# Half of the gate projections of a hybrid transformer layer, in pairs by one level of Strassen's method

## The chip, the cores and the metric

The kernel runs on one core of a Trainium2 chip. The metric is the device time of one execution in microseconds; lower is better. Engines are called by short names: PE (TensorE, matrix products), DVE (VectorE), ACT (ScalarE), POOL (GpSimd) and SP (SyncE, which issues the DMAs here).

## The reference

One layer on x of 1024 positions x 1024 channels, in float32. Cut to what matters here:

```python
proj = x @ w_in
q_a, k_a, v_a, f_a, q_b, f_b, i_b, g_b, gate_a, gate_b = split(proj)
y_a = fox_attention(q_a, k_a, v_a, log_sigmoid(f_a + b_f))       # 8 heads of 64
o_b = hgrn2_chunkwise(silu(q_b), 1 - f, i_b, log(f))             # 4 heads of 128, f from f_b
o_b = o_b * rsqrt(mean(o_b ** 2) + eps) * norm_g
y_b = o_b * sigmoid(g_b)
merged = sigmoid(gate_a) * (y_a @ w_pa) + sigmoid(gate_b) * (y_b @ w_pb)
x = layer_norm(ALPHA * x + merged @ w_o)
u, g = split(x @ w_ff_in)                                        # 2 x 2816 wide
x = layer_norm(ALPHA * x + (silu(g) * u) @ w_ff_out)
```

The change concerns gate_a and gate_b: two products of x (1024 x 1024) with a weight matrix of 1024 x 1024.

## The kernel before

Every product of float32 matrices is made of three matmuls on parts of reduced width: both factors are split into a high part, a cast on ACT, and a low part, the difference, on DVE (`split`, L337). `mm3` (L366) issues high x high, high x low and low x high into one PSUM bank. A matmul takes a 128x128 piece of a weight as the stationary operand and 512 positions of x^T as the moving one, so its result is a tile of 128 channels x 512 positions. The split parts of x^T (xh, xl) stay in SBUF from the start.

The stages are: the accumulations for v (va, vb); the projections and the attention of four pairs of heads; the projections and the recurrence of four heads of HGRN2 (`hgrn`, L613); the branch projections p_a and p_b with the merge (tiles pps); w_o and the first layer norm; the FFN; the second layer norm. The FFN already computes its first product by one level of Strassen's method (`chunk`, L1043): for two column blocks of 128 channels and two halves of 512 positions, seven products of half the contraction length with sums of operands, instead of eight. Its split weight parts (tiles Tp) rotate over six slots: four of tag kb, and wr0 and wr1 (TSLOTS, L975).

The gates are 16 projections: two sets (i = 0 for gate_a, 1 for gate_b) of KC = 8 blocks of 128 channels. `gate(n, lane)` (L766) does one: it loads the block's weights (tile wg_r, 512 KB), splits them in two parts of four k-chunks (wg_h, wg_l), runs `project` (L377) for either half of the positions, 8 chunks x 3 matmuls each into a bank gps, copies the bank to SBUF on ACT (tile gt) and stores it to gate_d in DRAM. The merge loads it back later (tile sg).

The order of everything is a planner's. The program first records all calls in the class Plan (L54 to L280), with the tiles that each needs. `schedule` then lists them greedily: at each step the call that can start earliest by the planner's own costs goes next, with ties to the one recorded first; a tile's slot must be free. `issue` emits the result at one line, which is why every row of the profile names L280. The gates are recorded last, behind the recurrence (L790), so those of set 0 go into PE's holes during attention and recurrence, and those of set 1 run one behind the other after the recurrence's last head. LATE (L29) gives the gates 8, 10, 12 and 14 lane 0 (weight tiles wr0, wh0, wl0 and bank g), the others lane 1 (bank h).

At the end of a head's recurrence (L741 to L762) the chain is: nb (the decays of the last level, DVE), a matmul lp_nb, two COPY_PREDICATED of the mask into the matrix at (DVE), the matmuls op, the squares with their sums on ACT (ob, ss), ss scaled on DVE, rr = ss to the power -1/2 on POOL, ob = op x rr on DVE, four transposes ot on PE, yb on DVE, and the store to yb_d. It is run for two halves.

Of the kernel before, what the change touches and what calls it, by code (L numbers as in the profile page):

```python
# [8 lines left out]
F32R = mybir.dt.float32r  # L9
# [7 lines left out]
P = 128  # L17
S = 1024
D = 1024
KC = D // P  # L20
# [3 lines left out]
NB = 512  # L24
# [1 line left out]
CHUNKS = [[(0, n)] if n <= NB else [(0, n - w), (n - w, w)] for n, w in  # L26
          ((128, 0), (256, 0), (384, 0), (512, 0), (640, 256), (768, 256), (896, 384), (1024, 512))]
WTAGS = ("qk",) * 6 + ("kb",) * 4 + ("pf",) * 4 + ("hl",) * 2
LATE = (8, 10, 12, 14)  # L29
MERGE = {"g": "s"}  # L30
SPREAD = {"s": 2, "pt": 2, "pv": 1, "g": 1, "h": 2}
LOOSE = ("ps_s", "gt", "ps_h")
# [251 lines left out]
def trunk(ctx: ExitStack, tc, a: dict, out: bass.AP):  # L284
    nc = tc.nc
    plan = Plan(tc)
    sync, act, dve, pool, pe = (plan.queue(n, e) for n, e in (
        ("SP", nc.sync), ("ACT", nc.scalar), ("DVE", nc.vector), ("POOL", nc.gpsimd), ("PE", nc.tensor)))
# [13 lines left out]
    def bank(tag, name):  # L302
        tag = MERGE.get(tag, tag)
        return plan.tile(ps, [P, NB], F32, "ps_" + tag, name, BANKS[tag])

    def take(tag, shape, name, dt=F32):
        return plan.tile(root, [P] + shape, dt, tag, name, BUFS[tag])

    def full(tag, name, dt=F32):
        return take(tag, [S], name, dt)  # L310

    def half(tag, name, dt=F32):
        return take(tag, [NB], name, dt)
# [14 lines left out]
    def hs(i):  # L328
        return slice(i * NB, (i + 1) * NB)
# [4 lines left out]
    def f(ap):  # L334
        return ap.bitcast(F32)

    def split(hi, lo, src):  # L337
        act.copy(hi, src)
        dve.tensor_sub(lo, src, f(hi))
# [3 lines left out]
    def lane_of(lane):  # L343
        if lane is None:
            lane = turn[0]
            turn[0] ^= 1
        return lane
# [6 lines left out]
    def weights(src, shape, name, lane=None):  # L354
        lane = lane_of(lane)
        raw = raw_load(src, shape, name, lane)

        n = shape[0] // 2
        parts = []
        for i in range(2):  # L360
            hi, lo = (take(f"w{x}{lane}", [n] + shape[1:], f"{name}_{x}{i}", F32R) for x in "hl")
            split(hi, lo, raw[:, i * n:(i + 1) * n])
            parts.append((hi, lo))
        return [tuple(t[:, c % n] for t in parts[c // n]) for c in range(shape[0])]

    def mm3(o, lh, ll, rh, rl, first, last, more={}):  # L366
        mm(o, lh, rh, start=first, stop=False, **more)
        mm(o, lh, rl, start=False, stop=False, **more)
        mm(o, ll, rh, start=False, stop=last, **more)

    xh = [take("x", [4, S], f"xh{i}", F32R) for i in range(2)]
    xl = [take("x", [4, S], f"xl{i}", F32R) for i in range(2)]

    def X(c):
        return xh[c // 4][:, c % 4, :], xl[c // 4][:, c % 4, :]
# [10 lines left out]
    stage = ["qk"] * 6 + ["kb"] * 2  # L386
# [3 lines left out]
    for c2 in range(KC // 2):  # L390
# [12 lines left out]
        lane = lane_of(None)  # L403
        for j in range(2):
            c = 2 * c2 + j
            wh, wl = (take(f"w{n}{lane}", [NB], f"wva{c}_{n}", F32R) for n in "hl")
            h, l = X(c)
# [27 lines left out]
    for t in range(NT):  # L435
        vb = half(("tt", "ph")[t % 2], f"vb{t}")
        o = [bank(("pt", "h")[t % 2], f"vb_acc{t}_{i}")[:, :HV] for i in range(2)]
        for i in range(2):
            r = slice(i * HV, (i + 1) * HV)
            for c in range(KC):  # L440
                h, l = X(c)
# [322 lines left out]
    gate_d = dram.tile([2, KC, P, S], F32, name="gate_d")  # L764

    def gate(n, lane):  # L766
        i, fb = divmod(n, KC)
        plan.early = EARLY
        w = weights(a["w_g"][i, fb], [KC, P], f"wg{i}_{fb}", lane)
        plan.early = 0  # L770
        for hf in range(2):
            o = bank("gh"[lane], f"gps{i}_{fb}_{hf}")
            project(o, w, hf)
            t = half("gt", f"gt{i}_{fb}_{hf}")
            act.copy(t, o)
            sync.dma_start(gate_d[i, fb, :, hs(hf)], t)

    qk = qk_project(0)
    for p in range(4):
        attention(p, qk)  # L780
        if p < 3:
            qk = qk_project(p + 1)
# [3 lines left out]
    for h in range(HB):  # L786
        hgrn(h, qfg, box)
        if h < HB - 1:
            qfg = hgrn_project(h + 1)
    for n in range(2 * KC):  # L790
        gate(n, 0 if n in LATE else 1)


    UTAGS = ["qk"] * 6 + ["hl"] * 2 + ["kb"] * 4 + ["pf"] * 4
# [7 lines left out]
    for i, src in enumerate((ya_d, yb_d)):  # L802
# [6 lines left out]
        for fb in range(KC):  # L809
# [4 lines left out]
            w = [(hi[:, c], lo[:, c]) for c in range(4)]  # L814
            for hf in range(2):
# [3 lines left out]
                o = bank(CYC[nbank % 5], f"pps{i}_{fb}_{hf}")  # L819
# [92 lines left out]
    for t in range(NT):  # L912
# [16 lines left out]
        for g in range(2):  # L929
# [3 lines left out]
            if t < 4:  # L933
                h, l = (X11, X12)[g]
# [61 lines left out]
    class Chunk:  # L996
        def __init__(self, c, raw=None):
            self.c = c
            self.g, self.u = raw or (take("pf", [KC, P], f"w{n}{c}_r") for n in "gu")
            for i, t in enumerate((self.u, self.g)):  # L1000
                sync.dma_start(t, a["w_ff"][c, i])
            self.r = {}

        def sums(self, *names):
            g, u = self.g, self.u
            b11, b12, b21, b22 = g[:, :4], u[:, :4], g[:, 4:], u[:, 4:]
            for n in names:
                self.r[n] = take("tt", [4, P], f"t{n}_{self.c}")
                x, y = {"1": (b12, b11), "2": (b22, self.r.get("1")), "3": (b22, b12), "4": (b21, self.r.get("2"))}[n]
                dve.tensor_sub(self.r[n], x, y)  # L1010
# [15 lines left out]
    def mul(k, n, o, first, apart=False):  # L1026
        product(o, k.T(n, apart), OPS[n], first)
# [75 lines left out]
    for k, o in zip(ks, banks):  # L1103
        k.sums("3")
        mul(k, "p7", o[1], False)
        u3 = ring(f"u3_{k.c}")
# [51 lines left out]
    u = [half(("wh0", "wl0", "wh1", "wl1")[i], f"fu{i}") for i in range(4)]  # L1158
# [4 lines left out]
    for prod in ("p1", "p5", "p6", "p4", "p7", "p2"):  # L1163
# [3 lines left out]
        for g in range(len(GR)):  # L1167
            d, n = group(prod, ai[prod], g)
# [4 lines left out]
        for t in range(4):  # L1173
            o = acc[t]
# [29 lines left out]
    for t in range(4):  # L1204
# [5 lines left out]
        for i, s_ in enumerate(parts):  # L1210
            w = s_.stop - s_.start
            o = next_bank(f"p3_{t}_{i}")
# [100 lines left out]
```

## Time and profile before

| | |
|---|---|
| time, median of 3 runs | 1484.45 us (1484.18 to 1487.03) |
| the profiled execution | 1483.79 us |
| its span | 1482.0 us |
| mean granted PE clock | 0.998 |
| PE busy | 1464.2 us, 99% |
| DVE busy | 1005.8 us, 68% |
| ACT busy | 648.7 us, 44% |
| gates behind the recurrence | 569.65 to 656.80 us |

The profiled execution is one run of the program with the hardware profiler; its times belong together and lie near the median. A busy share is over the whole span. Matmuls overlap their neighbours, so the time that one adds is read from the starts of a dense row of them, not from the length of its record.

### The profile page before, as it was taken

The numbers are of one execution on the slowest core, as the hardware profiler recorded it, in microseconds if no ns is written. First come the engines' busy times: TensorE is split into PE (matmuls) and PEld (weight loads), VectorE is DVE, ScalarE is ACT, GpSimd is POOL, SyncE is SP. The second block draws the span as 40 slices with busy tenths as digits, with TensorE's granted clock in tenths as the row PEclk, the third lists the DMA queues.
The fourth block names the chain that finished last, engine by engine and source line by source line (L and its number), as shares of the span: only waits on it lengthen the run. The fifth ranks groups of instructions, "written<-read, shape, count | busy, mean of one in ns | idle before, by whom it ended". The sixth has DMA issues, their size and how long they took to land.

```text
span 1482.0 us, 19306 instructions
## 1 busy us (share of the span) xinstructions
PE 1464.2 (99%) x7081; PEld 1218.4 (82%) x7081; DVE 1005.8 (68%) x1913; ACT 648.7 (44%) x1101; POOL 95.6 (6%) x116
## 2 busy tenths in 40 slices
PE   9999999999999999999999899999999999999998
PEld 7997888888887888888888778888888888888887
DVE  5238676686887882134838897666666666798597
ACT  5127667677567653234511443233332333434330
POOL 0004132130101000000001000000000000000000
PEclk9999999999999999999999999999999999999999
DMA  6202212121211214346710304222233335976741
GB/s 241 77 33 83 69 55 77 42 75 40 78 36 57 67 63 142 107 157 222 265 52 1 114 22 136 97 95 98 102 106 107 107 107 175 342 265 226 250 160 58
DMA packets 78415, 170.68 MB, mean 115 GB/s; under 512 B 7400, under 2 KB 20328, under 8 KB 78320
## 3 DMA queue, kind: packets, MB, share of 16 engines
q1 hardware_dynamic: 78320, 169.44, 34.1%
q8 instruction: 56, 0.92, 0.3%
q14 instruction: 39, 0.32, 0.1%
HBM read 130.32 MB, written 39.09 MB: 114 GB/s over the span
## 4 chain that ended last, share of the span: by engine, by line
PE 94%; DVE 3%; ACT 1%; DMA 1%; issue 0%; POOL 0%; SPq 0%; DVEq 0%; ACTq 0%
PE p L280 14%; PE fb L280 11%; PE gps L280 11%; PE fc L280 8%; PE fa L280 8%; PE bps L280 8%; PE pps L280 6%; PE o L280 6%; PE vb_acc L280 3%; PE va_acc L280 3%; PE pv L280 2%; PE s L280 2%; PE qps L280 2%; PE kps L280 2%; PE pt L280 2%; PE lp L280 1%
## 5 line engine op out<-in xcount | busy, mean ns | idle before, releaser
L280 PE MATMUL p<-dp 128*128 128x512 f32 (+1 forms) x957 | 210.0, 382 | 0.0
L280 PEld LDWEIGHTS p<-dp 128*128 128x128 f32 x957 | 175.4, 188 | 34.7
L280 PE MATMUL fc<-xs,Tp 128*128 128x512 f32 x528 | 127.1, 390 | 0.0
L280 PE MATMUL fb<-xs,Tp 128*128 128x512 f32 x528 | 126.7, 390 | 0.0
L280 PEld LDWEIGHTS fc<-xs,Tp 128*128 128x128 f32 x528 | 99.1, 188 | 20.7 <-ACT xs L280 0.2
L280 PEld LDWEIGHTS fb<-xs,Tp 128*128 128x128 f32 x528 | 99.1, 188 | 20.6
L280 PE MATMUL fa<-x,Tp 128*128 128x512 f32 x480 | 115.8, 390 | 0.3 <-DVE u L280 0.3
L280 PEld LDWEIGHTS fa<-x,Tp 128*128 128x128 f32 x480 | 90.1, 188 | 19.3 <-ACT p L280 0.7
L280 ACT CAST Tp<-t 128x512 fp32r<-128x512 f32 x88 | 54.3, 620 | 116.4 <-PE fc L280 71.9
L280 DVE TENSOR_TENSOR Tp<-t,Tp 128x512 fp32r<-128x512 f32 x88 | 60.6, 691 | 60.5 <-ACT Tp L280 60.0
L280 PE MATMUL gps<-xl,wg_h 128*128 128x512 f32 x256 | 101.4, 396 | 0.0
L280 PE MATMUL gps<-xh,wg_h 128*128 128x512 f32 x256 | 101.3, 396 | 0.0
L280 PE MATMUL gps<-xh,wg_l 128*128 128x512 f32 x256 | 100.9, 394 | 0.0
L280 ACT CAST dp<-dap 128x1024 fp32r<-128x1024 f32 (+1 forms) x42 | 41.2, 983 | 102.2 <-PE p L280 51.7
L280 PE MATMUL bps<-xh,wb_l 128*128 128x512 f32 x192 | 76.1, 397 | 0.0
L280 PE MATMUL bps<-xh,wb_h 128*128 128x512 f32 x192 | 76.0, 396 | 0.0
L280 PE MATMUL bps<-xl,wb_h 128*128 128x512 f32 x192 | 75.9, 396 | 0.0
L280 POOL TENSOR_TENSOR rstd<-ve,mhalf 128x1 f32<-128x1 f32 x16 | 14.6, 914 | 898.1 <-DVE ve L280 898.1
L280 DVE TENSOR_TENSOR tl<-pt,th 128x512 fp32r<-128x512 f32 (+1 forms) x96 | 50.7, 552 | 20.2 <-ACT th L280 20.0
L280 DVE TENSOR_TENSOR wg_l<-wg_r,wg_h 128x512 fp32r<-128x512 f32 x32 | 22.5, 704 | 57.8 <-ACT wg_h L280 57.8
L280 DVE TENSOR_TENSOR dp<-dap,dp 128x1024 fp32r<-128x1024 f32 (+1 forms) x42 | 47.5, 1133 | 15.2 <-ACT dp L280 15.2
L280 PE MATMUL fb<-x,Tp 128*128 128x512 f32 x240 | 57.7, 389 | 0.0
(282 smaller groups left out, 3339.8 us busy)
## 6 DMA issues: line engine op xcount, KB each, us to landing
dbp<-in_w_fo SPq DMA_DIRECT2D x45, 512.0 KB, 5.2
dap<-a_d SPq DMA_DIRECT2D x35, 512.0 KB, 4.6
a_d<-ar SPq DMA_DIRECT2D x42, 256.0 KB, 3.8
wu_r<-in_w_ff SPq DMA_DIRECT2D x20, 512.0 KB, 3.7
wg_r<-in_w_ff SPq DMA_DIRECT2D x20, 512.0 KB, 3.6
a_d<-as SPq DMA_DIRECT2D x33, 256.0 KB, 2.3
wg_r<-in_w_g SPq DMA_DIRECT2D x16, 512.0 KB, 3.6
gate_d<-gt SPq DMA_DIRECT2D x32, 256.0 KB, 2.4
```

The source lines that it names most:

```text
L280: getattr(q.engine, method)(*args, **kw)
```

## The change

The first 8 gates (PLAIN) stay as they were, all of them in lane 1. The other 8 are taken in four pairs of neighbouring blocks. With g and u the weights of the two blocks of a pair and q the quarters of x^T (two halves of the contraction, two halves of the positions), one level of Strassen's method (the variant with shared sums, as in the FFN) gives the four result tiles from seven products of 4 chunks x 3 matmuls. A product's weight operand is a sum of quarters of g and u (tiles tg, on DVE) or a quarter itself; it is split into Tg..h (ACT) and Tg..l (DVE), in the tiles of the old gates' weight parts (tags wh0, wl0, wh1, wl1, two buffers each). The lanes alternate from product to product. The moving operand of p1, p2 and p4 is a quarter of xh, xl. For p5, p6, p7 and p3 the sums of quarters (gs1 to gs4) are made anew: x^T is loaded again in eight pieces of 512 KB (xg), added on DVE and split. The pairs 8 and 12 of the weights are named by their first block. The pairs 8 and 10 are worked jointly, product by product; the sums of x^T are made between. The pairs 12 and 14 follow in the FFN's order of products. The results are combined by copies on ACT (gp1, gt) and additions on DVE (gp1, gu2, gu3) and stored to gate_d as before.

```diff
@@ -26,7 +26,7 @@
 CHUNKS = [[(0, n)] if n <= NB else [(0, n - w), (n - w, w)] for n, w in
           ((128, 0), (256, 0), (384, 0), (512, 0), (640, 256), (768, 256), (896, 384), (1024, 512))]
 WTAGS = ("qk",) * 6 + ("kb",) * 4 + ("pf",) * 4 + ("hl",) * 2
-LATE = (8, 10, 12, 14)
+PLAIN = 8
 MERGE = {"g": "s"}
 SPREAD = {"s": 2, "pt": 2, "pv": 1, "g": 1, "h": 2}
 LOOSE = ("ps_s", "gt", "ps_h")
@@ -787,8 +787,144 @@
         hgrn(h, qfg, box)
         if h < HB - 1:
             qfg = hgrn_project(h + 1)
-    for n in range(2 * KC):
-        gate(n, 0 if n in LATE else 1)
+    for n in range(PLAIN):
+        gate(n, 1)
+    def operand4(tags, name):
+        ts = [[take(tags[2 * j + i], [2, NB], f"{name}{'hl'[i]}{j}", F32R) for j in range(2)] for i in range(2)]
+        return [[ts[i][c // 2][:, c % 2, :] for c in range(4)] for i in range(2)]
+    def operand1(tag, name):
+        t = take(tag, [2, 4, NB], name, F32R)
+        return [[t[:, i, c, :] for c in range(4)] for i in range(2)]
+    def quarter(i, m):
+        return [[x[i][:, c, hs(m)] for c in range(4)] for x in (xh, xl)]
+    gops = {"p1": quarter(0, 0), "p2": quarter(1, 0), "p4": quarter(1, 1)}
+    glane = [0]
+    class GatePair:
+        def __init__(self, n):
+            self.n = n
+            self.at = [divmod(n + j, KC) for j in range(2)]
+            self.w = []
+            for j in range(2):
+                t = take("kb", [KC, P], f"wg{n + j}_r")
+                sync.dma_start(t, a["w_g"][self.at[j]])
+                self.w.append(t)
+            (g, u), self.r = self.w, {}
+            self.src = {"p1": g[:, :4], "p2": g[:, 4:], "p3": u[:, 4:]}
+        def sums(self, *names):
+            g, u = self.w
+            for n in names:
+                t = take("tt", [4, P], f"tg{n}_{self.n}")
+                self.r[n] = t
+                x, y = {"1": (u[:, :4], g[:, :4]), "2": (u[:, 4:], self.r.get("1")), "3": (u[:, 4:], u[:, :4]),
+                        "4": (g[:, 4:], self.r.get("2"))}[n]
+                dve.tensor_sub(t, x, y)
+                self.src[{"1": "p5", "2": "p6", "3": "p7", "4": "p4"}[n]] = t
+        def mul(self, p, o, first):
+            lane = glane[0]
+            glane[0] ^= 1
+            T = [take(f"w{x}{lane}", [4, P], f"Tg{p}_{self.n}{x}", F32R) for x in "hl"]
+            split(*T, self.src[p])
+            more = {} if first else {"skip_group_check": True}
+            A = gops[p]
+            for c in range(4):
+                mm3(o, T[0][:, c], T[1][:, c], A[0][c], A[1][c], first and c == 0, c == 3, more)
+        def store(self, j, hf, t):
+            i, fb = self.at[j]
+            sync.dma_start(gate_d[i, fb, :, hs(hf)], t)
+        def stage(self, o):
+            t = half("gt", f"gt{self.n}_11")
+            act.copy(t, o)
+            self.store(0, 0, t)
+    pairs = [GatePair(n) for n in (PLAIN, PLAIN + 2)]
+    gbanks = [[bank(t, f"gs{k.n}_{i}") for i, t in enumerate(tags)] for k, tags in zip(pairs, (("h", "s", "s", "h"), ("s", "pv", "pt", "pt")))]
+    xr = []
+    for c in range(4):
+        two = [full(("wr0", "wr1")[j] if c == 0 else "qk", f"xg{c + 4 * j}_r") for j in range(2)]
+        for j in range(2):
+            sync.dma_start(two[j], a["xT"][c + 4 * j])
+        xr.append(two)
+    q11, q21, q12, q22 = ([x[j][:, hs(m)] for x in xr] for j, m in ((0, 0), (0, 1), (1, 0), (1, 1)))
+    def sums4(op, dst, x, y, sub):
+        for c in range(4):
+            (dve.tensor_sub if sub else dve.tensor_add)(dst[c], x[c], y[c])
+            split(op[0][c], op[1][c], dst[c])
+    for k, o in zip(pairs, gbanks):
+        k.mul("p1", o[0], True)
+        k.p1 = half("ph", f"gp1_{k.n}")
+        act.copy(k.p1, o[0])
+        k.mul("p2", o[0], False)
+        k.stage(o[0])
+        k.sums("1", "2", "4")
+        k.mul("p4", o[3], True)
+    gops["p5"] = operand1("x", "gs1")
+    sums4(gops["p5"], q22, q21, q22, False)
+    for k, o in zip(pairs, gbanks):
+        k.mul("p5", o[2], True)
+    gops["p6"] = operand1("m", "gs2")
+    sums4(gops["p6"], q22, q22, q11, True)
+    for k, o in zip(pairs, gbanks):
+        k.mul("p6", o[1], True)
+        k.u2 = half("ph", f"gu2_{k.n}")
+        dve.tensor_add(k.u2, o[1], k.p1)
+    gops["p7"] = operand4(("pf",) * 4, "gs3")
+    sums4(gops["p7"], q11, q11, q21, True)
+    for k, o in zip(pairs, gbanks):
+        k.sums("3")
+        k.mul("p7", o[1], False)
+        dve.tensor_add(k.p1, o[1], k.p1)
+        u3 = half("tt", f"gu3_{k.n}")
+        dve.tensor_add(u3, o[3], k.p1)
+        k.store(0, 1, u3)
+        dve.tensor_add(k.p1, o[2], k.p1)
+        k.store(1, 1, k.p1)
+    gops["p3"] = operand1("v", "gs4")
+    sums4(gops["p3"], q12, q12, q22, True)
+    for k, o in zip(pairs, gbanks):
+        k.mul("p3", o[2], False)
+        dve.tensor_add(k.u2, o[2], k.u2)
+        k.store(1, 0, k.u2)
+    G8 = ("h", "s", "s", "s", "h", "pt", "pv", "pt")
+    gb = 0
+    for n in range(PLAIN + 4, 2 * KC, 2):
+        k = GatePair(n)
+        ka, kb, kc = (bank(G8[(gb + i) % 8], f"gs{n}_{i}") for i in range(3))
+        gb += 3
+        p1, u2, u3 = (half("ph", f"g{x}_{n}") for x in ("p1", "u2", "u3"))
+        k.mul("p1", ka, True)
+        act.copy(p1, ka)
+        k.sums("1", "2")
+        k.mul("p6", kb, True)
+        dve.tensor_add(u2, kb, p1)
+        k.mul("p5", kc, True)
+        k.sums("3")
+        k.mul("p7", kb, False)
+        k.mul("p2", ka, False)
+        dve.tensor_add(u3, kb, p1)
+        k.sums("4")
+        k.mul("p4", kb, False)
+        dve.tensor_add(u3, kc, u3)
+        k.store(1, 1, u3)
+        k.stage(ka)
+        k.mul("p3", kc, False)
+        dve.tensor_add(p1, kb, p1)
+        k.store(0, 1, p1)
+        dve.tensor_add(u2, kc, u2)
+        k.store(1, 0, u2)
 
 
     UTAGS = ["qk"] * 6 + ["hl"] * 2 + ["kb"] * 4 + ["pf"] * 4
```

**The tail of the last head's recurrence, on DVE.** Before, the rows from the last difference nbp3 to the second ob3 are these (names end in the number of the buffer; wg0_7 are the weight parts of gate 7):

```order
L280 TENSOR_TENSOR nbp3_1285<-nbp3_1285,nbe3_1286 128x512
L280 TENSOR_TENSOR nb3_1284<-nbp3_1285,nb3_1284 128x512
L280 TENSOR_TENSOR wg0_7_l0_1365<-wg0_7_r_1363,wg0_7_h0_1364 128x512
L280 COPY_PREDICATED at3_1254<-lmask_172,lp3_nb_1287 128x4x64 x2
L280 TENSOR_TENSOR wg0_7_l1_1367<-wg0_7_r_1363,wg0_7_h1_1366 128x512
L280 TENSOR_SCALAR ss_1289<-ss_1289 128x4
L280 TENSOR_TENSOR ob3_0_1290<-op3_0_1288,rr_1291 128x512
L280 SCALAR_TENSOR_TENSOR yb3_0_1293<-ot3_0_1292,ng_173,hbg3_1228 128x512
L280 TENSOR_SCALAR ss_1295<-ss_1295 128x4
L280 TENSOR_TENSOR ob3_1_1296<-op3_1_1294,rr_1297 128x512
```

Now the piece up to the second part of the mask reads:

```order
L280 TENSOR_TENSOR gs1_1414<-xg5_r_1387,gs1_1414 128x512
L280 TENSOR_TENSOR nb3_1284<-nbp3_1285,nb3_1284 128x512
L280 TENSOR_TENSOR xg6_r_1389<-xg2_r_1388,xg6_r_1389 128x512
L280 TENSOR_TENSOR xg5_r_1387<-xg5_r_1387,xg1_r_1386 128x512
L280 TENSOR_TENSOR wg0_7_l0_1365<-wg0_7_r_1363,wg0_7_h0_1364 128x512
L280 COPY_PREDICATED at3_1254<-lmask_172,lp3_nb_1287 128x4x64
L280 TENSOR_TENSOR gs1_1414<-xg6_r_1389,gs1_1414 128x512
L280 COPY_PREDICATED at3_1254<-lmask_172,lp3_nb_1287 128x4x64
```

and the piece behind it, up to the first ob3:

```order
L280 TENSOR_TENSOR xg6_r_1389<-xg6_r_1389,xg2_r_1388 128x512
L280 TENSOR_TENSOR xg1_r_1386<-xg1_r_1386 128x512
L280 TENSOR_TENSOR wg0_7_l1_1367<-wg0_7_r_1363,wg0_7_h1_1366 128x512
L280 TENSOR_TENSOR xg2_r_1388<-xg2_r_1388 128x512
L280 TENSOR_TENSOR gs3l0_1428<-xg1_r_1386,gs3h0_1426 128x512
L280 TENSOR_TENSOR xg5_r_1387<-xg5_r_1387 128x512
L280 TENSOR_SCALAR ss_1289<-ss_1289 128x4
L280 TENSOR_TENSOR xg6_r_1389<-xg6_r_1389 128x512
L280 TENSOR_TENSOR ob3_0_1290<-op3_0_1288,rr_1291 128x512
L280 TENSOR_TENSOR xg4_r_1385<-xg0_r_1384,xg4_r_1385 128x512
```

Additions on the reloaded x^T (xg) and its sums (gs1, gs3l0) have come between the steps of the recurrence, and another one stands between ss and ob.

**The first product of pair 12, on PE.** Before, one gate follows another as here, at the end of gate 1 of set 1 and the start of gate 2; their weight parts were split while the gate ahead ran:

```order
L280 MATMUL gps1_1_1_1388<-xh1_67,wg1_1_l1_1385 128x512
L280 MATMUL gps1_1_1_1388<-xh1_67,wg1_1_h1_1384 128x512
L280 MATMUL gps1_1_1_1388<-xl1_69,wg1_1_h1_1384 128x512
L280 MATMUL gps1_1_1_1388<-xh1_67,wg1_1_l1_1385 128x512
L280 MATMUL gps1_2_0_1395<-xh0_66,wg1_2_h0_1391 128x512
L280 MATMUL gps1_2_0_1395<-xl0_68,wg1_2_h0_1391 128x512
L280 MATMUL gps1_2_0_1395<-xh0_66,wg1_2_l0_1392 128x512
L280 MATMUL gps1_2_0_1395<-xh0_66,wg1_2_h0_1391 128x512
```

Now, where the product p7 of pair 8 (bank gs8_1) ends, the first product of pair 12 (bank gs12_0) begins:

```order
L280 MATMUL gs8_1_1377<-gs3h1_1427,Tgp7_8l_1432 128x512
L280 MATMUL gs8_1_1377<-gs3h1_1427,Tgp7_8h_1431 128x512
L280 MATMUL gs8_1_1377<-gs3l1_1429,Tgp7_8h_1431 128x512
L280 MATMUL gs8_1_1377<-gs3h1_1427,Tgp7_8l_1432 128x512
L280 MATMUL gs12_0_1445<-xh0_66,Tgp1_12h_1451 128x512
L280 MATMUL gs12_0_1445<-xl0_68,Tgp1_12h_1451 128x512
L280 MATMUL gs12_0_1445<-xh0_66,Tgp1_12l_1452 128x512
```

On ACT the casts of these products' weights stand in this order (yh03 is a cast for the stage behind the gates):

```order
L280 CAST Tgp7_8h_1431<-tg3_8_1430 128x512
L280 CAST yh03_1513<-yr03_r_1512 128x1024
L280 CAST Tgp3_8h_1439<-wg9_r_1373 128x512
L280 CAST Tgp1_12h_1451<-wg12_r_1443 128x512
L280 CAST Tgp7_10h_1435<-tg3_10_1434 128x512
L280 CAST Tgp3_10h_1441<-wg11_r_1375 128x512
```

The product p1 of pair 12 was put ahead of p7 of pair 10 and p3 of pair 8; of its 12 matmuls the first ten run here, and the last two some thirty rows later.

## Rows read from the trace of the kernel before

**Rows 1.** The page: span, busy time by engine, shares of the chain that ended last

```profile
span 1482.0 us, 19306 instructions
...
PE 1464.2 (99%) x7081; PEld 1218.4 (82%) x7081; DVE 1005.8 (68%) x1913; ACT 648.7 (44%) x1101; POOL 95.6 (6%) x116
...
PE 94%; DVE 3%; ACT 1%; DMA 1%; issue 0%; POOL 0%; SPq 0%; DVEq 0%; ACTq 0%
```

**Rows 2.** Waits of PE: total us, times, longest us

```profile
PE fa L280 <- ACT Tp_0h L280: 4.1, 1, 4.1
PE ot L280 <- DVE ob L280: 1.6, 1, 1.6
```

**Rows 3.** Windows: us; busy PE, PEld, DVE, ACT, POOL; clock; DMA share; GB/s

```profile
400.00:420.00 20.00, 19.26 (x88) 15.73 (x87) 13.70 (x24) 18.01 (x28) 2.06 (x1) 1.00 0.23 70
...
840.00:860.00 20.00, 17.79 (x73) 14.06 (x74) 18.76 (x34) 12.54 (x22) 0.92 (x1) 0.91 0.23 94
920.00:1240.00 320.00, 320.00 (x1413) 265.11 (x1412) 222.27 (x337) 99.86 (x168) 0.00 (x0) 1.00 0.32 107
569.65:656.80 87.15, 87.15 (x386) 72.20 (x385) 15.89 (x20) 24.02 (x40) 0.00 (x0) 1.00 0.37 125
544.00:570.00 26.00, 26.00 (x141) 21.57 (x140) 13.82 (x30) 10.14 (x29) 2.01 (x2) 1.00 0.42 137
```

**Rows 4.** The chain: start us, us, what, count

```profile
566.26 90.70 PE gps L280 x400
```

**Rows 5.** Timeline of PE: start us, us, the instruction

```profile
569.76 0.39 PE L280 MATMUL gps<-xh,wg_h 128*128 128x512 f32 x1
...
656.80 0.39 PE L280 MATMUL pps<-yh,wp_h 128*128 128x512 f32 x1
```

**Rows 6.** Groups in 569.7 to 656.8 us: busy us, mean ns, idle before

```profile
L280 DVE TENSOR_TENSOR wg_l<-wg_r,wg_h 128x512 fp32r<-128x512 f32 x13 | 9.0, 693 | 52.9 <-ACT wg_h L280 52.9
L280 ACT CAST wg_h<-wg_r 128x512 fp32r<-128x512 f32 x13 | 8.1, 623 | 23.6 <-PE gps L280 23.6
```

**Rows 7.** Timeline, tail of head 3's recurrence; in brackets idle time and releaser

```profile
551.58 0.69 DVE L280 TENSOR_TENSOR nb<-nbp,nb 128x512 fp32r<-128x512 f32 x1 [0.69 <-ACT nb L280]
552.18 0.68 DVE L280 TENSOR_TENSOR wg_l<-wg_r,wg_h 128x512 fp32r<-128x512 f32 x1
552.86 1.30 DVE L280 COPY_PREDICATED at<-lmask,lp_nb 128x256 f32<-128x256 uint16 x2
...
554.22 0.49 PE L280 MATMUL op<-box,at 128*128 128x128 f32 x2
...
557.30 0.22 ACT L280 ACTIVATION_READ_ACCUMULATOR ob<-op 128x1 f32 x1
...
557.94 1.01 POOL L280 TENSOR_TENSOR rr<-ss,mhalf 128x4 f32<-128x4 f32 x1 [43.63 <-DVE ss L280]
558.98 0.69 DVE L280 TENSOR_TENSOR ob<-op,rr 128x512 f32<-128x512 f32 x1 [1.18 <-POOL rr L280]
...
559.76 0.63 PE L280 MATMUL ot<-ident,ob 128*128 128x128 f32 x4
```

**Rows 8.** Groups in the FFN, 920 to 1240 us: an addition from PSUM

```profile
L280 DVE TENSOR_TENSOR u<-fb,p 128x512 f32<-128x512 f32 x34 | 23.5, 692 | 26.0 <-PE fb L280 26.0
```

**Rows 9.** The page, DMA issues: KB each, us to landing

```profile
wg_r<-in_w_g SPq DMA_DIRECT2D x16, 512.0 KB, 3.6
```

**Rows 10.** Timeline, the tail of an earlier head's recurrence

```profile
401.25 1.23 DVE L280 TENSOR_TENSOR box<-hbb 128x1024 f32<-128x1024 f32 x1
401.29 2.06 POOL L280 TENSOR_TENSOR rr<-ss,mhalf 128x4 f32<-128x4 f32 x1 [3.95 <-DVE tot L280]
...
404.22 0.63 PE L280 MATMUL ot<-ident,ob 128*128 128x128 f32 x4 [0.74 <-DVE tot L280]
```

**Rows 11.** Timeline, a weight tile handed over between two gates

```profile
577.47 0.39 PE L280 MATMUL gps<-xl,wg_h 128*128 128x512 f32 x1
...
577.90 0.62 ACT L280 CAST wg_h<-wg_r 128x512 fp32r<-128x512 f32 x1 [1.86 <-PE gps L280]
```

## The prediction

> **What bounds the kernel now.** I read the page first: TensorE (PE) is busy for 1464.2 of 1482.0 us, and the chain of work that ended last runs through PE for 94% of the span [rows 1]. The waits of PE come next: the longest that it makes for another engine is 4.1 us, the next 1.6, and the windows have none in the stretch that is changed [rows 2, 3]. Then the windows: from 569.65 to 656.80 us PE is busy for all of 87.15 us, VectorE (DVE) for 15.89 and ScalarE (ACT) for 24.02; from 920 to 1240 us, where the FFN's Strassen products run, PE is busy for 320 of 320 us although DVE carries 222.27 [rows 3]. The chain itself shows 90.70 us of gate matmuls in one piece [rows 4]. So a matmul that goes from this stretch shortens the kernel by its step, as long as DVE, ACT and the loads keep up with what is left.
>
> **What the change removes.** The gates behind the recurrence are 8 blocks x 2 halves x 8 k-chunks x 3 = 384 matmuls. They run from 569.76 to the first pps at 656.80 us [rows 5], which is 87.04 / 384 = 0.2267 us each (a record's 0.39 us is longer because neighbours overlap). Four pairs of seven products with 4 k-chunks x 3 matmuls are 336. All have the same shape as before, so at the same step and a full clock the gain is 48 x 0.2267 = 10.9 us. The other eight gates stay as they are; they fill PE's holes in attention and recurrence.
>
> **What it adds, and what hides it.** On DVE 80 operations on 128x512 come on balance: 28 low parts of the products' weights, 16 sums of reloaded x with 16 low parts of them, 16 sums of weights, 20 additions to results, less 16 wg_l. One takes 0.69 us alone [rows 6]; back to back the step is 552.18 - 551.58 = 0.60 to 0.61 [rows 7]. The additions that read PSUM cost the same: u<-fb,p in the FFN is 692 ns [rows 8]. That is 80 x 0.61 = 49 us, against 71 us that DVE has free in the gate stretch and 12 us free from 544 to 570 [rows 3]. On ACT 28 + 16 casts and 8 copies come, 32 casts and copies go: 20 x 0.62 = 12 us, against 63 free. Eight loads of 512 KB come on SP; a load of a gate's weights of that size lands in 3.6 us [rows 9], and a core that moves 125 GB/s at a DMA share of 0.37 [rows 3] has room. On average all of it is covered; what counts is where each stands in its queue.
>
> The tightest piece is the first half. In the changed order DVE has 66 operations from gs1 ahead of nb3 up to gu2_10: 56 x 0.61 + 4 yl x 1.2 + 2 x 0.65 + 2 x 0.75 + 2 x 0.15 = 42 us, while PE has 219 matmuls from the first lp3_nb to gu2_10's products: 49.6 us. That is 85% of DVE's time, against 222.27 / 320 = 69% in the FFN.
>
> **First place: the tail of head 3's recurrence.** Before, nb on DVE is followed by one wg_l and then the two COPY_PREDICATED of the mask, which end at 552.86 + 1.30 = 554.16; PE's op takes up the second half at 554.22 [rows 7]. In the new order xg6 and xg5 stand ahead of them, and a gs1 between them: the second half ends at 551.58 + 0.69 + 3 x 0.61 + 0.65 + 0.61 + 0.65 = 556.0, which is 1.85 later (the gs1 ahead of nb fits into the 0.69 us in which DVE waits there). PE has 8 gate matmuls more to run between the first lp3_nb and that op, 1.8 us, which just about covers it; where a step is 0.69 instead of 0.61 it does not, so I take 0.3. Then comes the chain op, squares on ACT, ss on DVE, rr on GpSimd, ob on DVE, ot on PE. Before, 18 gate matmuls (4.1 us) cover it, and ot shows no wait but also no slack: ob begins at 558.98, ends at 559.67 and ot stands at 559.76 [rows 7]. After, it is 18 again, and six DVE operations are queued between the mask and ss: 556.0 + 6 x 0.61 = 559.7 against 557.52 + 1.85 = 559.4 at which the squares are done. Behind ss stands another xg6. So ot3_0 comes 0.6 late, and ot3_1, covered by one matmul more, 0.3. Queued behind are yb3_0, yb3_1 and their stores to yb_d, which nobody needs for 80 us. Sum of the place: 0.3 + 0.6 + 0.3 = 1.2 us. Bounds: 0 if DVE's steps are hidden as wg_l is before; 4.1 if a late reload (xg4 and xg7 are issued only after the stores of gate 6) holds ss up as Tp_0h holds fa [rows 2].
>
> Of the 0.6 and 0.3, 0.5 each hang on rr. At 401.29 rr took 2.06 us where the sum box<-hbb on DVE had begun at 401.25 and read two SBUF tiles; at 557.94, with no such neighbour, 1.01; and ot at 404.22 then waited 0.74 [rows 7, 10]. The Trainium skill ("SBUF — State Buffer", section "Who interferes with whom") says that a DVE instruction with two SBUF inputs contends with a GpSimd instruction that reads SBUF, and that whoever issues first blocks the other for its whole length. The trace agrees: 2.06 - 1.01 = 1.05 us is nearly what was left of box's 1.23. By the rule the xg6 behind ss3_0 (0.69 us, begun shortly ahead of rr) adds about half a microsecond to each rr; without it the place would cost 0.4 rather than 1.2.
>
> **Second place: the first product of pair 12.** Each product's weights are split into four tiles, which are two buffers for either lane. gs12_0 stands right behind gs8_1's p7 and takes the buffer of a product that ended just before: its cast Tgp1_12h can start only when the last but one p7 matmul has read the old tile. How long such a handover takes, the old gates show: the matmul that starts at 577.47 ends at 577.86, and the cast starts at 577.90 and takes 0.62 [rows 11]. PE has one matmul (0.23) for that: 0.39 + 0.04 + 0.62 - 0.23 = 0.8 us of waiting, and the low part, queued behind gp1_8 on DVE, about 0.4 more: 1.2 us. The ends are 0 (the buffer came free a product earlier) and 1.7 (both casts and low part in a row, 0.62 + 0.69 + 0.39).
>
> **The rest.** p2_8 behind the copy gp1_8, p3_10 behind its chain over gu3_8, and p4_10 behind the cast yh00 have slacks within 0.3 us of nothing; I take 0.3 for all three together, with 0 and 1.5 as ends. From pps on PE's work stands as before.
>
> **The sum.** -10.9 + 1.2 + 1.2 + 0.3 = -8.2 us. The profiled execution took 1483.79 us (span 1482.0 and 1.8 around it); it would come to 1475.6. The median of the runs shown is 1484.45, 0.7 above the profiled one, so I predict 1476.3. With the lower ends 1473.6, with the upper ends (4.1 + 1.7 + 1.5) 1480.9. A wait also risks the clock: after the 4.11 us ahead of fa the window 840 to 860 has a granted clock of 0.91, but 400 to 420, with its wait of 0.74, stays at 1.00 [rows 3]. My waits are like the latter, so I add nothing.
>
> **Rivals.**
> 1. *All of it hidden.* The planner leaves room for its operations, and DVE is 69% busy beside a full PE in the FFN [rows 3]. Then it is 1484.45 - 10.9 = 1473.6. Against it: the two places above, where the order itself puts work between a step and who waits for it.
> 2. *DVE late as a whole.* In the first half it is 85% loaded. If its operations take 0.69 instead of 0.61, each waiting for a cast or a load, that is 56 x 0.08 = 4.5 us more, 47 of 49.6 us, and any wait for a cast of ACT goes through to PE. Then the places cost twice to three times as much, 7 to 11 us: 1481 to 1484.5, no change that can be told. For it: before, DVE's gate operations did wait for ACT each time [rows 6]. Against it: they waited because ACT in turn waited for PE.
> 3. *Slower: every product waits for its weights.* Four T buffers stand where the FFN has six. Break-even is 10.9 / 28 = 0.39 us for a product; if each of the 28 waited as I expect of gs12_0, 0.8 to 1.2 us, the result is +11.5 to +22.7 us, 1496 to 1507; if half of them did so at 0.9, 12.6 - 10.9 = +1.7, 1486. It decides from the point where the buffer's last reader is less than 0.39 + 0.04 + 0.62 + 0.69 = 1.74 us ahead of the product, that is, where it is the product just before. Against it: lanes alternate and have two buffers each, so between the last reader and the next user of a buffer there are normally three products, 3 x 12 x 0.2267 = 8.2 us; only where products of two pairs interleave does the order break that.
> 4. *The clock falls in the gate stretch* after a wait of about 4 us. At 0.91 over 20 us [rows 3] that costs 1.8 us on top of the wait: 1480 to 1482.
>
> **Chances.** My forecast with its bounds 0.68, rival 1 0.15, rival 2 0.09, rival 3 0.04, rival 4 0.04. No change means within 0.2% or 3 us, which is what a measurement here can tell. Faster takes my forecast, rival 1 and half of rival 4, with a part of rival 2: 0.88; no change 0.08; slower 0.04. The range 1473.2 to 1480.9 reaches from rival 1 to the upper ends and leaves out rivals 2 and 3 and part of 4.
>
> **What would show it.** Right: 48 gate matmuls fewer with the same 0.227 us step between the recurrence and pps; waits of op, ot and gs12_0 on PE, for at, ob and Tgp1_12h, of 0.3 to 0.8 us each; rr of about 1.5 us in head 3; a clock of 1.00. Wrong: waits for Tgp tiles at most products (rival 3), a DVE share near 95% from 551 to 600 us with waits for gs or tg tiles (rival 2), or a slower granted clock.

## The result

| | median, us | runs | before in the same comparison | ratio, 95% interval |
|---|---|---|---|---|
| changed kernel | 1475.47 (1474.88 to 1476.22) | 4 | 1484.32 (4 runs) | 0.9937 [0.992, 0.9955] |
| the same, a second time | 1476.65 (1475.79 to 1477.29) | 5 | 1484.77 (9 runs) | 0.9944 [0.9931, 0.9958] |

The change takes 8.9 us off in the first comparison and 8.1 in the second. The forecast was 8.2 us less, 1476.3; the two medians lie 0.8 below it and 0.4 above it. The profiled execution took 1476.22 us. Its page, as [rows 1]:

```profile
span 1474.4 us, 19347 instructions
...
PE 1455.1 (99%) x7033; PEld 1208.2 (82%) x7033; DVE 1053.3 (71%) x1993; ACT 659.8 (45%) x1121; POOL 96.6 (7%) x116
...
PE 93%; DVE 4%; ACT 1%; DMA 1%; issue 0%; POOL 0%; SPq 0%; DVEq 0%; ACTq 0%; POOLq 0%
```

DVE is busy for 47.5 us more (49 forecast at its back-to-back step) and PE has 48 matmul records fewer. The waits of PE, as [rows 2] (total us, times, longest):

```profile
PE fa L280 <- ACT Tp_0h L280: 4.1, 1, 4.1
PE ot L280 <- DVE ob L280: 1.6, 1, 1.6
...
PE gs L280 <- ACT Tgp_12h L280: 0.5, 1, 0.5
...
PE gs L280 <- DVE Tgp_12l L280: 0.2, 1, 0.2
```

The two large ones stand where they stood; from the tail of the recurrence to pps only the two for the weights of gs12_0 are new. The windows, as [rows 3] (busy PE, PEld, DVE, ACT, POOL; clock; DMA share; GB/s), are the gate products and the stretch from the tail of the recurrence to about the end of p7 of pair 8:

```profile
551.00:600.00 49.00, 48.77 (x231) 39.50 (x230) 41.43 (x66) 25.49 (x55) 2.63 (x2) 1.00 0.54 181
571.25:649.10 77.85, 77.12 (x338) 62.71 (x337) 50.89 (x79) 30.12 (x49) 0.00 (x0) 1.00 0.41 138
```

The clock stays at its full level; DVE is busy for 41.43 / 49 = 85% of the first, as the prediction had worked out from the order. The chain, as [rows 4] (start us, us, what), has the gate products in three pieces:

```profile
571.41 29.99 PE gs L280 x132
602.77 5.34 PE gs L280 x22
610.90 38.33 PE gs L280 x168
649.23 87.04 PE pps L280 x384
```

The breaks before 602.77 and before 610.90 are the waits. The first is the handover of a weight tile, as [rows 11]:

```profile
601.00 0.39 PE L280 MATMUL gs<-gs3h,Tgp_8l 128*128 128x512 f32 x1
601.20 0.62 ACT L280 CAST Tgp_12h<-wg_r 128x512 fp32r<-128x512 f32 x1 [4.82 <-PE gs L280]
601.43 0.69 DVE L280 TENSOR_TENSOR gp<-gs,gp 128x512 f32<-128x512 f32 x1 [2.03 <-PE gs L280]
601.87 0.50 PE L280 MATMUL gs<-xh,Tgp_12h 128*128 128x512 f32 x1 [0.48 <-ACT Tgp_12h L280]
602.03 0.68 DVE L280 TENSOR_TENSOR Tgp_12l<-wg_r,Tgp_12h 128x512 fp32r<-128x512 f32 x1
...
602.77 0.50 PE L280 MATMUL gs<-xh,Tgp_12l 128*128 128x512 f32 x1 [0.17 <-DVE Tgp_12l L280]
```

PE starts its last p7 matmul at 601.00; the next would follow at 601.23 and follows at 601.87, because ACT's cast can start only at 601.20. gp ahead of the low part on DVE delays the third matmul. The tail of the recurrence, as [rows 7]:

```profile
552.01 1.29 DVE L280 TENSOR_TENSOR xg_r<-xg_r 128x512 f32<-128x512 f32 x2
553.21 0.69 DVE L280 TENSOR_TENSOR wg_l<-wg_r,wg_h 128x512 fp32r<-128x512 f32 x1
553.82 0.73 DVE L280 COPY_PREDICATED at<-lmask,lp_nb 128x256 f32<-128x256 uint16 x1
554.33 0.73 DVE L280 TENSOR_TENSOR gs<-xg_r,gs 128x512 fp32r<-128x512 f32 x1
554.98 0.72 DVE L280 COPY_PREDICATED at<-lmask,lp_nb 128x256 f32<-128x256 uint16 x1
...
559.13 0.17 DVE L280 TENSOR_SCALAR ss<-ss 128x4 f32<-128x4 f32 x1
559.21 0.69 DVE L280 TENSOR_TENSOR xg_r<-xg_r 128x512 f32<-128x512 f32 x1
559.45 1.31 POOL L280 TENSOR_TENSOR rr<-ss,mhalf 128x4 f32<-128x4 f32 x1 [44.46 <-DVE ss L280]
560.79 0.69 DVE L280 TENSOR_TENSOR ob<-op,rr 128x512 f32<-128x512 f32 x1 [0.90 <-POOL rr L280]
561.63 0.63 PE L280 MATMUL ot<-ident,ob 128*128 128x128 f32 x4
```

The sums xg stand ahead of wg_l and the mask, a gs between the two parts of the mask, as forecast, and rr runs beside an xg. The list of waits names neither op nor ot of this tail: a matmul's record of 0.39 us is longer than its step and covers most of the gap (the start before ot's 561.63 is at 561.10).

So to weigh such places I take the time from one PE start to another and subtract 0.2267 us for each matmul that the order has between. What is left is an excess (a little under zero where transposes or 128-wide matmuls step faster); only differences between columns mean something:

| excess, us | before | changed | second time | e1 | e2 | e7 | e9 |
|---|---|---|---|---|---|---|---|
| first lp3_nb to op3_0 | 0.25 | 0.36 | 0.36 | 0.36 | 0.20 | 0.21 | 0.19 |
| op3_0 to ot3_0 | 0.22 | 0.68 | 0.68 | 0.68 | 0.37 | 0.36 | 0.36 |
| ot3_0 to ot3_1 | -0.44 | -0.20 | 0.59 | -0.20 | -0.43 | -0.43 | 0.42 |
| ot3_1 to pps | -0.46 | 1.27 | 1.28 | -0.35 | 3.76 | 0.59 | -0.34 |

From lp3_nb to pps the change adds 2.11 + 0.43 = 2.5 us of excess. Of the 48 matmuls 43 go from this stretch and 5 from ahead of it, 10.9 us in all; together that is -8.3 us. The two profiled executions differ by 7.6 us. Most of the remaining 0.8 stands ahead of lp3_nb, 0.5 of it at the start of the program, where PE waits 0.8 us for the first xh instead of 0.3; in the second profile of the changed kernel that wait is not there.

### The profile page after: what moved, and what is told of

The parts are those of the page before. It is cut to its first block, busy times and chain, and to the rows that moved or that the text cites. A ratio compares the mean times of both kernels' runs of the same rounds, so it can differ in the third digit from the quotient of the medians.

```text
span 1474.4 us, 19347 instructions
## 1 busy us (share of the span) xinstructions
PE 1455.1 (99%) x7033; PEld 1208.2 (82%) x7033; DVE 1053.3 (71%) x1993; ACT 659.8 (45%) x1121; POOL 96.6 (7%) x116
## 4 chain that ended last, share of the span: by engine, by line
PE 93%; DVE 4%; ACT 1%; DMA 1%; issue 0%; POOL 0%; SPq 0%; DVEq 0%; ACTq 0%; POOLq 0%
PE p L280 14%; PE fb L280 11%; PE fc L280 8%; PE fa L280 8%; PE bps L280 8%; PE pps L280 6%; PE o L280 6%; PE gs L280 5%; PE gps L280 5%; PE vb_acc L280 3%; PE va_acc L280 3%; PE kps L280 3%; PE pv L280 2%; PE s L280 2%; PE qps L280 2%; PE pt L280 2%
## 5 line engine op out<-in xcount | busy, mean ns | idle before, releaser
L280 DVE TENSOR_TENSOR dp<-dap,dp 128x1024 fp32r<-128x1024 f32 (+1 forms) x42 | 47.5, 1134 | 15.4 <-ACT dp L280 15.4
L280 POOL TENSOR_SCALAR p<-p,rs 128x128 f32<-128x128 f32 (+3 forms) x64 | 47.5, 749 | 140.7 <-DVE rs L280 91.0
L280 ACT CAST th<-pt 128x512 fp32r<-128x512 f32 (+1 forms) x96 | 43.2, 479 | 28.3 <-PE pt L280 27.1
L280 ACT ACTIVATE p<-p,nm 128x128 f32<-128x128 f32 (+3 forms) x64 | 49.5, 776 | 9.0 <-DVE nm L280 8.5
L280 PEld LDWEIGHTS fb<-x,Tp 128*128 128x128 f32 x240 | 45.1, 188 | 9.4
```

The source lines that it names most:

```text
L280: getattr(q.engine, method)(*args, **kw)
```

## The experiments

Theory: the gain is the 48 matmuls at their step, less two places (the tail, the buffer of gs12_0); all other added work is covered. Rivals: the new order or lanes give a part of the gain; VectorE is near its limit; each product pays for its few weight buffers.

**The same kernel again** (no edit).

> The changed kernel once more, as the base of the runs beside it. Theory: 48 matmuls fewer at 0.227 us less about 2.3 us of waits in the stretch from the last lp_nb to pps, so 8.5 us less than before, 1475.5 to 1476. If the first comparison was lucky in its before or after, the difference would be under 7.

Measured: 1476.65 us, 8.1 below before and 0.65 above the range expected. The tail differs from the first profile in one place, the second half. The first profile had there:

```profile
566.04 0.69 DVE L280 TENSOR_TENSOR tg<-wg_r,tg 128x512 f32<-128x512 f32 x1
566.28 1.31 POOL L280 TENSOR_TENSOR rr<-ss,mhalf 128x4 f32<-128x4 f32 x1 [5.52 <-DVE ss L280]
566.64 0.69 DVE L280 TENSOR_TENSOR gs<-xg_r,gs 128x512 fp32r<-128x512 f32 x1
567.62 0.69 DVE L280 TENSOR_TENSOR ob<-op,rr 128x512 f32<-128x512 f32 x1 [0.30 <-POOL rr L280]
```

and the second has:

```profile
565.39 0.68 DVE L280 TENSOR_TENSOR tg<-wg_r,tg 128x512 f32<-128x512 f32 x1
565.62 1.92 POOL L280 TENSOR_TENSOR rr<-ss,mhalf 128x4 f32<-128x4 f32 x1 [5.70 <-DVE ss L280]
565.99 0.69 DVE L280 TENSOR_TENSOR gs<-xg_r,gs 128x512 fp32r<-128x512 f32 x1
567.57 0.69 DVE L280 TENSOR_TENSOR ob<-op,rr 128x512 f32<-128x512 f32 x1 [0.90 <-POOL rr L280]
```

In both, rr starts 0.23 or 0.24 us behind tg, and gs 0.60 behind tg; still rr took 1.31 us in the one and 1.92 in the other. What decides between the two lengths these rows do not show; it stays open. So the price of the tail is 0.8 us in the one and 1.6 in the other.

**e1, both sums tg3 recorded ahead of both p7 products.**

```diff
+    for k in pairs:
+        k.sums("3")
     for k, o in zip(pairs, gbanks):
-        k.sums("3")
         k.mul("p7", o[1], False)
```

> The two sums tg3_8 and tg3_10 are recorded ahead of both p7 products, so that tg3_10 no longer queues for a tile behind gu3_8; then p7 of pair 10 stands right behind p7 of pair 8 and gs12_0 comes later, with its buffer free long before. Theory (the waits of 0.64 + 0.11 + 0.33 + 0.11 at gs12_0 come from the handover of one buffer from the product just before): they go, about 1.2 us less than the changed kernel, and no wait for Tgp_12h or Tgp_12l is left. Rival (four buffers for 28 products are too few and the wait only moves to the next product): some other Tgp tile is waited for by 0.5 us or more and the time stays within 0.3 us.

Measured: 1474.49 us (1473.43 to 1474.98), ratio to before 0.993 [0.9918, 0.9942]; 2.2 us less than the changed kernel beside it. PE has no wait at all between 500 and 660 us, and the excess from ot3_1 to pps falls from 1.28 to -0.35. That is 1.6 rather than the 1.2 expected, mostly because the small wait of p3_10 (0.3) went with it. The rest of the difference between the two profiles is the tail, which had the short rr here; how often either length comes in the executions without a profile is not shown. The wait was the handover, and it moved nowhere else.

**e2, the sums of x late; e7, both edits; e9, late but only behind ob3_0.** The planner is given one more predecessor for these 16 sums: the multiplication ob3_1 (e9: ob3_0). e7 and e9 contain e1.

```diff
+            plan.last_ob = len(plan.calls)
             dve.tensor_mul(ob..., op..., rr...)
...
+            plan.after = plan.last_ob
             (dve.tensor_sub if sub else dve.tensor_add)(dst[c], x[c], y[c])
+            plan.after = None
```

> The 16 sums of the reloaded x may not be placed ahead of ob3_1, so none stands in VectorE's queue between the steps of the last head's tail. Theory: op3_0, ot3_0 and ot3_1 lose their 0.8 us of delay; rr in head 3 takes 1.01 us wherever no sum of two SBUF tiles runs beside it (a tg sum still may, behind ss3_1); VectorE then has the 16 sums with the products' work in the 40 us that follow, so p5 and p6 may wait: net between -0.8 and +3 us against the changed kernel. Rival (the 0.8 us are PE's own steps and switches, not VectorE's queue): ot3_0 and ot3_1 come as late as now.

> Both edits of the two runs beside it at once. Theory: the two waits are independent, so the gains add up: -2.0 us against the changed kernel, 1473.5, if the late sums cost nothing; if they do, this run shows the same loss as the run with late sums alone, less 1.2.

> Both tg3 sums early as in the run that gained 2 us, and the 16 sums of x held back only until ob3_0 (instead of ob3_1): the first half of the tail is free of them, and VectorE gets them 6 us earlier than when all were late. Theory: rr takes 1.01 us in the first half; in the second, where tg2_8 and gs1 with two SBUF inputs stand behind ss, 1.3 to 1.9; op3_0 and ot3_0 lose their 0.5 us; the 0.6 us that gs10_2 waited for gp with all sums late shrinks or goes. So 0.3 to 0.8 us below the run with the early tg3 sums alone, 1473.7 to 1474.2 on a chip where before takes 1484.8, 10.5 to 11.1 below before. Rival: VectorE is as late with the sums as before, the time is that of both edits, 10.6 below, and the 0.6 us wait is still there.

Measured: e2 1476.64 us, ratio 0.9944 [0.9931, 0.9956]; e7 1474.13, 0.9929 [0.9916, 0.9941]; e9 1474.09 (1473.7 to 1474.52), 0.9929 [0.9916, 0.9943]. In e2 and e7 the tail is back within 0.15 us of the excess of before (the table), so its delay was VectorE's queue and not PE's own steps. e2 pays for it at gs12_0, where Tgp_12l comes 1.1 us late (its edit adds a line, so its rows say L281):

```profile
600.11 0.50 PE L281 MATMUL gs<-xh,Tgp_12h 128*128 128x512 f32 x1 [0.48 <-ACT Tgp_12h L281]
601.94 0.51 PE L281 MATMUL gs<-xh,Tgp_12l 128*128 128x512 f32 x1 [1.10 <-DVE Tgp_12l L281]
...
602.89 0.63 PE L281 MATMUL gs<-xh,Tgp_12l 128*128 128x512 f32 x1
603.32 0.63 PE L281 MATMUL gs<-xh,Tgp_12h 128*128 128x512 f32 x1
```

```profile
603.00:605.00 2.00, 2.00 (x6) 1.54 (x5) 1.92 (x4) 1.14 (x2) 0.00 (x0) 0.50 0.83 325
```

Behind these two waits the matmuls step by 0.43 us, and the granted clock is 0.50, the lower of its two levels, until about 606. So of the 2.5 us by which the last row of the table lies above the changed kernel's, 0.9 are the longer wait and 1.6 the clock: nine steps from 602.51 to 606.16 take 3.65 us instead of 2.04. That eats the gain in the tail, and e2's time is that of the changed kernel. In e7 one wait is left, and the clock stays at 1.00:

```profile
607.37 0.74 PE L281 MATMUL gs<-gs,Tgp_10h 128*128 128x512 f32 x2 [0.64 <-DVE gp L281]
```

In e9 that wait is gone, and rr behaves as expected: 1.01 us in the first half, 1.92 in the second, where ot3_1 is late again (the table). The three versions e1, e7 and e9 lie within 0.4 us of each other, too near to be ranked, and 10.3 to 10.7 below before (e9 beside its own before), against 8.1 for the change beside e1 and e7: by the medians all of the 10.9 but 0.2 to 0.6 us. By the table each still has 0.9 to 1.2 us more excess than before, so a part of that closeness is the spread between executions.

**e3, the eighth product.** `mul` issues the 12 matmuls of p1 twice.

```diff
+            for turn in range(2 if p == "p1" else 1):
-            for c in range(4):
-                mm3(...)
+                for c in range(4):
+                    mm3(...)
```

> Each pair runs the 12 matmuls of its product p1 twice (the second run starts the bank anew, so the result is the same): 384 matmuls behind the recurrence as before, with all the added work of VectorE, ScalarE and the loads. Theory (the whole gain is matmuls left out, the added work costs only the waits found): 48 x 0.227 = 10.9 us more than the changed kernel, less at most 1.5 us where the longer p1 covers a wait: 1485 to 1487.5, that is 0 to 3 us above before. Rival (a part of the gain comes from the new order or the other lanes): it stays below before by 2 us or more.

Measured: 1486.82 us (10 runs), ratio 1.0017 [1.0008, 1.0027], 2.4 above before. With the matmuls back, nothing of the gain is left, and what stays is the price of the two places. The rival (order, lanes) is out.

**e8, the kernel before with all gates in lane 1** (`LATE = ()`).

> The kernel before with LATE empty: all 16 gates in lane 1 and bank h, none in pairs. It tells what the other part of the change, the lane of the gates 8 to 14, does by itself. Theory: the gates of one lane still have two buffers of half a gate's weights, 24 matmuls each, so nothing waits longer than before: within 1 us of before. Rival: it is a gain of 2 us or more, and a part of the change's gain is this.

Measured: 1489.13 us, ratio 1.0032 [1.002, 1.0044], 4.7 us slower; both theories missed. The chain shows the merge's first weights (wp_r) loaded only when yl has read the tile that the load needs:

```profile
653.51 1.24 DVE yl L280
654.75 0.02 issue
654.76 4.49 DMA wp_r<-in_w_p
659.26 0.02 issue
659.28 0.63 ACT wp_h L280
```

and the timeline what PE does then:

```profile
659.95 0.79 PE L280 MATMUL pps<-yh,wp_h 128*128 128x512 f32 x1 [3.14 <-ACT wp_h L280]
660.54 0.63 PE L280 MATMUL pps<-yl,wp_h 128*128 128x512 f32 x1
660.97 0.63 PE L280 MATMUL pps<-yh,wp_h 128*128 128x512 f32 x1
```

The wait is 3.1 us, and behind it the matmuls step by 0.43 us until about 663: the granted clock is 0.92 from 660 to 680, where 81 matmuls start instead of 90. 9 x 0.2267 = 2.0 us, and 3.1 + 2.0 is about the loss. So the lanes are no source of the gain; in the change the pairs keep their weights in other tiles (kb), and pps waits for nothing.

**e4, more work for VectorE.** Each of the 16 low parts of the sums is computed twice, or three times.

```diff
             split(op[0][c], op[1][c], dst[c])
+            dve.tensor_sub(op[1][c], dst[c], f(op[0][c]))
```

> Each of the 16 low parts of the sums of x is computed twice: 16 more operations on VectorE, 9.8 us. From 551 to 600 us it was busy for 41.4 of 49 us in the changed kernel; 51 would be more than there is. Theory (the first half is the tight one; rival 2 of the prediction sets in where VectorE is full): PE waits there for gs or Tgp tiles, 2 to 6 us more than the changed kernel. Rival (VectorE's work is spread by the planner and hidden until pps): within 1 us of the changed kernel.

> The same with each low part three times: 32 operations more, 19.5 us, 61 us of work for the stretch of 49. Theory: 10 to 16 us more than the changed kernel, that is the whole gain is eaten, 1486 to 1492; the step from the run with one repeat to this one is near 32 - 16 = 16 operations x 0.61 = 9.8 us. Rival (hidden): within 3 us of the changed kernel.

Measured: 1478.06 us, ratio 0.9958 [0.9943, 0.9973], and 1482.18 us (10 runs), 0.9987 [0.9978, 0.9996]: 1.4 to 2.6 and 5.5 to 6.7 above the changed kernel's two medians, at or below the low end of the first range and about half of the second, so neither expectation holds for three. DVE is then busy throughout (windows of the run with three):

```profile
575.00:600.00 25.00, 25.00 (x112) 20.57 (x111) 25.00 (x42) 10.38 (x18) 0.00 (x0) 1.00 0.19 64
600.00:625.00 25.00, 21.44 (x84) 16.29 (x83) 24.08 (x40) 8.91 (x14) 0.00 (x0) 0.93 0.50 154
```

PE is still full from 575 to 600 us: the low parts that are needed late (gs2 to gs4) move back, to 611.9 us instead of 585.7, and the waits come where the results of p7 and p3 are handed round (2.27 us for gp at 604.97). So VectorE's limit is near, but 13 of the 19.5 us were hidden where up to 600 us only 49 - 41.4 = 7.6 were free. Behind the 2.27 us wait, which follows one of 0.5 after two matmuls, the clock fell again (0.93 in the window). With one repeat the waits in this stretch are 0.5 us and, ten us later, 1.0, and the clock stays at 1.00. A smaller part of the cost is in the tail, where rr takes 1.92 us in both halves of both runs.

**e5, fewer weight buffers.** The products of the pairs 12 and 14 keep to lane 1; in the second run a spare tile takes every other buffer.

```diff
-            lane = glane[0]
+            lane = glane[0] if self.n < 12 else 1
...
+            if self.n >= 12:
+                for x in "hl":
+                    spare = take(f"w{x}{lane}", [4, P], ...)
+                    pool.memset(spare[:, 0, :8], 0.0)
```

> All products of the pairs 12 and 14 take lane 1, so they have two weight buffers instead of four. The last reader of a buffer is then two products back, with one product of 12 x 0.227 = 2.72 us between; the handover takes 0.39 + 0.04 + 0.62 + 0.69 = 1.74 us. Theory: still covered, within 1 us of the changed kernel. Rival 3 of the prediction in its wider form (too few buffers make each product wait): 14 products wait for 0.4 us or more, 6 us and up.

> As the run beside it, and a spare tile that GpSimd only clears (8 elements) takes every second buffer, so that each of the 14 products of the pairs 12 and 14 must split its weights into the tile of the product just before. Theory (the price of a handover is the one seen at gs12_0, 0.64 + 0.11 + 0.33 + 0.11 = 1.19 us): 13 or 14 such waits, 15 to 17 us more than the changed kernel, slower than before by 6 to 9 us. Rival: the wait is partly hidden by work of another pair in between, or made longer by VectorE's queue (a sum ahead of a low part, 0.6 us each): 8 us, or 20 and more.

Measured: 1475.47 us, ratio 0.994 [0.9924, 0.9956], and 1475.28, 0.9941 [0.9923, 0.9959]; no cost in either, so the 15 to 17 us expected of one buffer did not come. But this is no verdict on the price of few buffers: in both runs the planner put matmuls of the merge (pps, whose gates of set 0 are long done) between the products, the first of them 204 matmuls earlier than in the changed kernel. What the runs show is that this stretch has work to fill with.

**e6, only two pairs** (`PLAIN = 12`).

> Only the gates 12 to 15 in two pairs, worked jointly with the sums of x; the gates 8 to 11 run as plain ones ahead of them. 24 matmuls fewer instead of 48. Theory: the gain of matmuls is half, 5.4 us; the sums of x (16, with 16 low parts) are all still needed but have 45 us of plain gates more to hide in, so the tail of the recurrence and the first products lose less: 4.5 to 5.4 us below before, 1479.4 to 1480.3. Rival (the sums cost the same wherever they stand): 3 us below before.

Measured: 1481.14 us (10 runs), ratio 0.9977 [0.9968, 0.9987], 2.9 below before, which is what the rival had. The tail (lp3_nb to ot3_1) has an excess of 1.1 us against 0.0 before, and pps waits 0.5 us for wp_h. The planner puts the sums as early as their loads allow, however much time there is behind them. That is 1.6 of the missing 2.5 us. The other 0.9 stands in the FFN, which the edit does not touch: in the profiled execution the time from the first fa to the end is 0.95 us longer than in that of before, with a clock of 0.77 in the window 830 to 845 (the last section shows what that is). The mean clocks on record say that more of its executions ran so: 0.996 in six of ten, against four of the twelve of before that are compared. At 0.996 the means are 1481.24 and 1484.99 us, 3.7 apart. So the rival's 3 us came out, but a part of the loss is not the sums.

## Why the prediction was right

**The step of the matmuls.** 10.9 us forecast; e3 shows it from the other side (1486.82 against 1475.47 and 1476.65, 10.2 to 11.4).

**The tail.** 1.2 us forecast as 0.3 + 0.6 + 0.3. Measured against before: 0.11 + 0.46 + 0.24 = 0.8, and 0.11 + 0.46 + 1.03 = 1.6 the second time. The mechanism was right (e2). The size of rr was not fixed at 1.5: in the two halves it was 1.31 and 1.31 the first time, 1.31 and 1.92 the second. The prediction lets "0.5 each" of the 0.6 and the 0.3 hang on rr, which is more than the second term holds. And of the waits that it named as signs, op's is 0.11 us of excess instead of 0.3 and no row of the list of waits. That the total of the forecast lies between the two medians is partly luck: 1.2 stands between two prices that one program shows.

**The port.** In two cases rr ends 0.86 or 0.87 us after the two-input operation of DVE beside which it was issued: 403.35 against 402.48 [rows 10], 560.76 against 559.90. In a third it ends 0.86 us after the next such operation, 567.54 against 566.68, and in the first profile's second half again after the one beside which it was issued, though another followed. Alone it takes 1.01. So it waits for the operation that DVE runs when it is issued, and sometimes for the next one too. The rule of the Trainium skill ("SBUF — State Buffer", "Who interferes with whom") holds in this direction. In the other one it does not show here: in e2 a DVE operation that began 0.21 us behind rr kept its 0.69 us, and rr its 1.01:

```profile
563.19 1.01 POOL L281 TENSOR_TENSOR rr<-ss,mhalf 128x4 f32<-128x4 f32 x1 [4.75 <-DVE ss L281]
563.40 0.69 DVE L281 TENSOR_TENSOR Tgp_8l<-tg,Tgp_8h 128x512 fp32r<-128x512 f32 x1 [0.36 <-ACT Tgp_8h L281]
```

**gs12_0.** 1.2 us forecast; 0.64 + 0.11 + 0.33 + 0.11 = 1.19 measured, and e1 takes it away. Its two parts are as forecast too: 0.8 for the cast and 0.4 for the low part, 0.75 and 0.44 measured.

**The rest.** 0.3 us forecast for three places; 0.24 + 0.09 = 0.33 at p3_10 alone, nothing at the others. The sum fits; that it stands at one of the three was not forecast.

**The rivals.** All hidden: not in the change, but e1, e7 and e9 come within 0.6 us of it by their medians. DVE late as a whole: its load was 85% as worked out, but e4 shows that even 16 operations more cost only about 2 us. Each product waits: one of 28 waited for its weights in the change; e5 does not test it. The clock: it did not fall in the gate stretch of the change; e8 shows what such a wait costs, 3.1 us and two more. But the prediction tied this to a wait of about 4 us, and e2 shows it behind waits of 0.48 and 1.10, for 1.6 us. The change with its 0.48 and 0.17 was nearer to it than the prediction took it to be.

## What to carry to other kernels

Where one engine runs without a gap, work saved on it comes off the time at its step, and the price of the new helpers is found by reading the order for two things: what has been queued between a step and who waits for it, and which tile's last reader is the product just before. A greedy planner places new helper work as early as it can, into a chain that has no slack, though it may be needed much later; a tile that a sum needs can be claimed in recorded order by something that is needed later (tg3 behind gu3), and recording it earlier gained 1.6 us here. Holding the sums back to spare one chain is not free either: in e2 it lengthened another wait, and the clock fell behind it.

## What the runs showed that I had not expected

The same program runs the start of the FFN in two ways: after the wait of 4.1 us for Tp_0h the granted clock, as a mean over the window from 830 to 845 us, is 0.89 in one execution and 0.77 in another (the changed kernel, first and second time):

```profile
830.00:845.00 15.00, 10.74 (x42) 8.45 (x43) 14.04 (x25) 9.79 (x17) 0.92 (x1) 0.89 0.47 189
```

```profile
830.00:845.00 15.00, 11.18 (x38) 8.73 (x39) 13.29 (x24) 9.47 (x17) 0.92 (x1) 0.77 0.46 182
```

Four matmuls fewer start in the second, 0.9 us, and from the first fa to the end it takes 0.9 us longer. With the two lengths of rr (0.8 us) this makes 1.7 us between executions of one program. The executions of the changed kernel lie up to 2.4 us apart (1474.88 to 1477.29), so these two places can make much of that; for the executions without a profile this is not shown. A difference of 1 us between two single traces says little until it is found at its place.
